# Compressed attention branch: three copies of the probabilities turned as one 128x128 piece, and one full-height product per query tile

## The chip, the cores and the metric

One NeuronCore of a Trainium2 chip runs the whole program. The metric is the device time of one execution in microseconds (us). Engines are named as the profile names them: PE (TensorE, matrix products and transposes; PEld is its weight load), DVE (VectorE), ACT (ScalarE), POOL (GpSimd), SP (SyncE, which issues most DMAs).

## The reference

Two layers over 256 tokens of width 2048: first an RWKV-7 mixer, then sparse attention with three branches (compressed, selected, window) over shared keys and values, each followed by an output product; a final norm ends it. The changed part is the compressed branch of the second layer: 16 heads in 4 groups, head width 128. Keys and values are compressed to 15 blocks, each query attends to the blocks that it can see, and the result is gated and added to the other branches:

```python
s = jnp.einsum('bgrqd,bgcd->bgrqc', qb, k_cmp).astype(jnp.float32) * scale      # c: 15 compressed blocks
vis = cmp_end[None, :] <= tq[:, None]
p_cmp = jax.nn.softmax(jnp.where(vis, s, NEG_INF), axis=-1) * jnp.any(vis, axis=-1)[:, None]
o_cmp = jnp.einsum('bgrqc,bgcd->bgrqd', p_cmp.astype(v_cmp.dtype), v_cmp)
...
o = gb[..., 0:1] * o_cmp + gb[..., 1:2] * o_sel + gb[..., 2:3] * o_win
```

With 256 tokens the selection takes all blocks, so the kernel computes the other two branches from the same causal scores with their own weights.

## The kernel before, in words

All products run in fp32r. An fp32 operand x is split into a high part (x rounded to fp32r by a copy on ACT) and a low part (x minus high, on DVE or POOL), and each product is the sum of three: high by high, high by low, low by high. Weights stream from DRAM through five raw buffers (line 176), are split on ACT (line 204) and on DVE or POOL (line 189), and are used by `rows_step` (lines 567 to 570; tokens stationary, up to 512 weight columns moving) and `cols_step` (lines 585 to 587; weights stationary, 256 tokens moving).

The stages in order: the RWKV layer; the shared keys and values (`phase_kv`, `compress`, buffers from the pool `kvp`); the attention stage, in which `phase_q` and `phase_z` stream the input weights while the attention of the heads runs beside them as a background generator; and the output product `phase_bo` with the final norm. When the attention stage opens, `kvp` is released and the pool `at` takes over its memory.

The order of instructions on each engine is not written by hand. The program is emitted in an order set by a small planner (`Sched`: each generator yields estimated costs in ns, and `sch.t` is the planned time), and the framework then orders each engine's queue by priority and by its own simulated time line. Calls through `Ranked` carry a priority offset; they all show as line 232 on PE, so their groups in the profile are told apart by tile names.

`compress(1, ...)` makes the compressed values: `vch` (high, ACT, line 1407) and `vcl` (low, DVE, line 1408), each 15 partitions by 4 groups by 128. `attend(p)` does one pair of heads, eight times, from pair 7 down to 0. For each head, `weigh` makes scores, exponentials (`P0`, `P1` for the causal scores, `Pc` for the compressed ones, two query tiles of 128 by 15) and scales them by gate and sum (lines 1527 to 1531). Then `turned` transposes four pieces into one PSUM bank and splits them into `Th` and `Tl` (512 columns: two heads by two query tiles by 128 queries), and `products` adds three products to the accumulator `o` (128 value rows by those 512 columns). T0, T1 and T2 serve the causal scores. T3 serves the compressed branch: four transposes of 128x15, `Th` and `Tl` of 15x512, and three products whose contraction has 15 rows:

```python
T3 = turned([Pc[:, t, 0:NCMP] for _, _, Pc in P for t in range(2)], NCMP)
...
products(o, (vch[:, g, :], vcl[:, g, :]), T3, stop=True)
```

Of the kernel before, what the change touches and what calls it, by code (L numbers as in the profile page):

```python
# [10 lines left out]
F32 = mybir.dt.float32  # L11
F32R = mybir.dt.float32r
AF = mybir.ActivationFunctionType
OP = mybir.AluOpType
# [9 lines left out]
NCMP = 15  # L24
GRP = 4
# [5 lines left out]
def _layout():  # L31
    p = np.arange(128)
    q = np.arange(64)
    f = {}
    f["ident"] = np.eye(128)
    f["bo"] = (p[:, None] // 64 == np.arange(2)[None])
    f["mi"] = (p % 64)[:, None] <= q[None]
    f["mst"] = (p % 64)[:, None] < q[None]
    f["rst"] = np.tile((np.arange(T) % CH != 0)[None], (128, 1))
    half_d = 16  # L40
    inv = (np.float32(500000.0) ** (-np.arange(half_d, dtype=np.float32) / np.float32(half_d))).astype(np.float32)
    pos = (np.arange(2)[None] * 128 + p[:, None]).astype(np.float32)
    ang = (pos[:, :, None] * inv[None, None]).astype(np.float32)
    f["cos"] = np.cos(ang.astype(np.float64)).reshape(128, 32)
    f["sin"] = np.sin(ang.astype(np.float64)).reshape(128, 32)
    angc = ((16.0 * (p % NCMP) + 31.0).astype(np.float32)[:, None] * inv[None]).astype(np.float32)
    f["ccos"] = np.cos(angc.astype(np.float64))
    f["csin"] = np.sin(angc.astype(np.float64))
    f["caus"] = np.where(p[None] <= p[:, None], 0.0, NEG)
    tt = np.arange(2)[None] * 128 + p[:, None]  # L50
    cend = 16 * np.arange(NCMP) + 31
    vis = cend[None, None] <= tt[:, :, None]
    f["vis"] = np.where(vis | ~vis.any(-1, keepdims=True), 0.0, NEG).reshape(128, 2 * NCMP)
    f["anyv"] = vis.any(-1)
    cols, parts, off = {}, [], 0
    for k, v in f.items():
        v = np.asarray(v, np.float32)
        cols[k] = (off, v.shape[1])
        parts.append(v)
        off += v.shape[1]  # L60
    return cols, np.ascontiguousarray(np.concatenate(parts, 1))
# [21 lines left out]
QTB, QB, PB, TB, OGB, RPB = 1, 8, 3, 3, 1, 1  # L83
# [132 lines left out]
def hybrid_kernel(ctx: ExitStack, tc: tile.TileContext, a: dict, out: bass.AP):  # L216
    nc = tc.nc
    V, S, G, PE = nc.vector, nc.scalar, nc.gpsimd, nc.tensor
    sch = Sched()
# [34 lines left out]
    def accp(name="acc"):  # L254
        n = turn.get(name, 0)
        turn[name] = n + 1
        b = role[name]
        return psum.tile([128, 512], F32, name=f"bank{b[n % len(b)]}", bufs=1)
# [104 lines left out]
    def C(name):  # L363
        o, n = COLS[name]
        return cst[:, o:o + n]
# [799 lines left out]
    for U in range(NU):  # L1165
        PBK[U] = pair_tile(U % 2)
        P = U - 1
# [54 lines left out]
    bp = kvp = xlp = None  # L1222
# [87 lines left out]
    KT = ktp.tile([128, GRP, 2, 272], F32, name="KT")  # L1310
    V.memset(KT[:, :, :, 256:], 0.0)
    Vt = [bp.tile([128, 2, GRP, 128], F32, name=f"Vt{i}") for i in range(2)]
    vcl = bp.tile([NCMP, GRP, 128], F32R, name="vcl")
    vch = bp.tile([NCMP, GRP, 128], F32R, name="vch")
    peT = bp.tile([128, 64], F32, name="peT")
    pt0 = accp("tp")
    PE.transpose(pt0[:, 0:64], perow, ident[:64, :64])
# [54 lines left out]
    def compress(j, o):  # L1372
        PE, V, S, G = Ranked(nc.tensor, "cpPE"), Ranked(nc.vector, "cpPE"), Ranked(nc.scalar, "cpPE"), Ranked(nc.gpsimd, "cpPE")
        t = kvp.tile([120, HID], F32, name="c1", bufs=1)
        S.activation(t, o, AF.Copy)
        pt = accp("tp")
        for m in range(2):
            PE.transpose(pt[:, m * 128:m * 128 + 120], t[:, m * 128:(m + 1) * 128], ident[:120, :120])
        yield 300.0
        p3 = pt[:, :256].rearrange("p (m c) -> p m c", m=2)  # L1380
        hs = kvp.tile([128, 2, 60], F32, name="c2", bufs=1)
        th = kvp.tile([128, 2, 60], F32, name="c3", bufs=1)
        S.activation(hs, p3[:, :, 60:120], AF.Copy)
        V.tensor_tensor(hs, p3[:, :, 0:60], hs, op=OP.add)
        S.activation(th, hs, AF.Tanh, scale=0.5)
        V.tensor_scalar(th, th, 0.5, 0.5, op0=OP.mult, op1=OP.add)
        V.tensor_tensor(hs, hs, th, op=OP.mult)
        yield 0.0
        o2 = accp("tp")
        if j == 0:  # L1390
            for m in range(2):
                PE.matmul(o2[:60, :128], hs[:, m, :], cw2[:, m, :], start=m == 0, stop=m == 1)
            kc = kvp.tile([128, 1, 1, 128], F32, name="kc", bufs=1)
            V.memset(kc, 0.0)
            S.activation(kc[:60, 0, 0, :], o2[:60, :128], AF.Copy)
            rope(kc, 1, C("ccos"), C("csin"), kvp, V)
            yield 0.0
            o3 = accp("tp")
            PE.transpose(o3[:, :60], kc[:60, 0, 0, :], ident[:60, :60])
            V.tensor_copy(KT[:, :, 0, 256:256 + NCMP], o3[:, :60].rearrange("p (g c) -> p g c", g=GRP))  # L1400
        else:
            for g in range(GRP):
                for m in range(2):
                    PE.matmul(o2[:NCMP, g * 128:(g + 1) * 128], hs[:, m, g * NCMP:(g + 1) * NCMP], cw2[:, 2 + m, :],
                              start=m == 0, stop=m == 1)
            vc = o2[:NCMP].rearrange("p (g d) -> p g d", g=GRP)
            S.activation(vch, vc, AF.Copy)
            V.tensor_tensor(vcl, vc, vch.bitcast(F32), op=OP.subtract)

    for ph in (phase_kv(0), phase_kv(2, 0), phase_kv(1), phase_kv(4, 1), phase_kv(3), phase_kv(5)):  # L1410
        sch.run(ph)
# [4 lines left out]
    at = tc.alloc_tile_pool(name="attn", bufs=1)  # L1416
# [5 lines left out]
    for tt in range(2):  # L1422
        rb = at.tile([128, 128], F32, name="rb", bufs=1)
        V.tensor_copy(rb, RS[tt].to_broadcast([128, 128]))
        PE.transpose(pr[:, tt * 128:(tt + 1) * 128], rb, ident)
    V.tensor_copy(RST, pr[:, :T])
    qd, zdone, kvd, used_q = {}, {}, {}, [0]

    def phase_q(n):
# [47 lines left out]
    def weigh(h):  # L1477
        PE, V, S, G = Ranked(nc.tensor, "atPE"), Ranked(nc.vector, "atE"), Ranked(nc.scalar, "atE"), Ranked(nc.gpsimd, "atE")
        g = h // GRP
# [28 lines left out]
        yield 500.0  # L1508
        P0 = at.tile([128, 2, 128], F32, name="P0", bufs=PB)
        P1 = at.tile([128, 2, 256], F32, name="P1", bufs=PB)  # L1510
        Pc = at.tile([128, 2, 16], F32, name="Pc", bufs=PB)
        for x in range(2):
            S.activation(P0[:, x], vA[:, x], AF.Exp, scale=SCALE, bias=mx[:, 0, x:x + 1], accum_out=sm[:, 0, x:x + 1])
        for t in range(2):
# [13 lines left out]
            V.tensor_scalar(P0[:, x], P0[:, x], rc[:, 0, x:x + 1], None, op0=OP.mult)  # L1528
            V.tensor_scalar(P1[:, x], P1[:, x], rc[:, 1, x:x + 1], None, op0=OP.mult)
        for t in range(2):  # L1530
            V.tensor_scalar(Pc[:, t, 0:NCMP], Pc[:, t, 0:NCMP], rc[:, t, 2:3], None, op0=OP.mult)
        yield 600.0
        return P0, P1, Pc

    def attend(p):
        PE, V, S, G = Ranked(nc.tensor, "atPE"), Ranked(nc.vector, "atE"), Ranked(nc.scalar, "atE"), Ranked(nc.gpsimd, "atE")
        g = p // 2
        if g not in kvd:
            split_kv(g)
        P = []  # L1540
        for h in (2 * p, 2 * p + 1):
            P.append((yield from weigh(h)))
        vh, vl = kvd[g][2:]

        def turned(pieces, n=128):
            pt = accp("PT")[:n]
            for i, piece in enumerate(pieces):
                PE.transpose(pt[:, i * 128:(i + 1) * 128], piece, ident)
            th = at.tile([128, 512], F32R, name="Th", bufs=TB)[:n]
            tl = at.tile([128, 512], F32R, name="Tl", bufs=TB)[:n]  # L1550
            S.activation(th, pt, AF.Copy)
            V.tensor_tensor(tl, pt, th.bitcast(F32), op=OP.subtract)
            sch.t += 430
            return th, tl

        def products(o, v, t, **kw):
            PE.matmul(o, v[0], t[0], start=kw.get("start", False), stop=False)
            PE.matmul(o, v[0], t[1], start=False, stop=False)
            PE.matmul(o, v[1], t[0], start=False, stop=kw.get("stop", False))

        T0 = turned([w for P0, P1, _ in P for w in (P0[:, 0], P1[:, 0, 0:128])])
        yield 500.0
        T1 = turned([w for P0, P1, _ in P for w in (P0[:, 1], P1[:, 1, 0:128])])
        yield 500.0
        if len(tails) >= OGB:
            yield lambda: ready(tails[0])
            yield from flush()
        o = accp("PV")
        os_ = o.rearrange("p (i s t) -> p i s t", i=2, s=2)[:, :, 1, :]
        products(o, (vh[:, 0, 0], vl[:, 0, 0]), T0, start=True)  # L1570
        T2 = turned([P1[:, x, 128:256] for x in range(2) for _, P1, _ in P])
        yield 500.0
        products(o, (vh[:, 1, 0], vl[:, 1, 0]), T1)
        T3 = turned([Pc[:, t, 0:NCMP] for _, _, Pc in P for t in range(2)], NCMP)
        yield 500.0
        for x in range(2):
            products(os_, (vh[:, x, 1], vl[:, x, 1]), [w[:, x * 256:(x + 1) * 256].rearrange("p (i t) -> p i t", i=2) for w in T2])
        products(o, (vch[:, g, :], vcl[:, g, :]), T3, stop=True)
        og = at.tile([128, 2, T], F32, name="og", bufs=OGB)
        S.activation(og, o.rearrange("p (i t) -> p i t", i=2), AF.Copy)  # L1580
        sch.t += 2600
        tails.append((p, og))
        yield 0.0
# [121 lines left out]
```

## Time and profile before

| | |
|---|---|
| runs before (us) | 1182.65, 1187.53, 1189.38; median 1187.53 |
| profiled execution: span from first to last instruction | 1181.0 us (the page gives no other time for it) |
| mean granted PE clock | 0.985 |
| PE busy | 1130.3 us (96%), 9416 instructions |
| DVE, ACT, POOL busy | 851.3 us (72%), 710.8 us (60%), 330.9 us (28%) |
| attention stage | from about 862 to 1085 us of the span |

How to read the profile's lines: a group shows line, engine, operation, output<-inputs by tile name, shape and count, then busy time and mean duration, and after the second bar the idle time of the engine just before, with what ended it. `bank` is any PSUM bank, `cst` the constants (the identity among them), `128*15` on a PE row the stationary operand's rows and columns and `128x512` the moving one's. In order of time a row begins with its start in the span and its length, in us. Matmuls overlap in these rows, since each is shown with its pipeline; how fast PE advances is read from start to start.

### The profile page before, as it was taken

The page shows a single profiled execution, that of the slowest core. Times are in us where ns is not written, and L with a number is a line of the kernel's source. Part 1 is how long each engine was busy: PE and PEld are TensorE (multiplying, and loading weights), DVE is VectorE, ACT ScalarE, POOL GpSimd, SP SyncE. Part 2 cuts the span into 40 slices and gives each one's busy share as a digit, 9 for nine tenths or more (in the row PEclk, how much of TensorE's full clock was granted, in tenths as well). Part 3 has the DMA queues.
Part 4 walks back from the last instruction along what each step waited for, and adds up shares of the span by engine and source line. Part 5 has one row for each costly group of instructions (what it writes and reads, how often), then busy time and mean ns, then how long its engine had stood idle before and what let it go on. Part 6 is the DMA issues. An engine that isn't in the chain of part 4 may idle for free.

```text
span 1181.0 us, 25607 instructions
## 1 busy us (share of the span) xinstructions
PE 1130.3 (96%) x9416; PEld 985.4 (83%) x9416; DVE 851.3 (72%) x1915; ACT 710.8 (60%) x1680; POOL 330.9 (28%) x413
## 2 busy tenths in 40 slices
PE   8999999999986999999989999999999999999997
PEld 7788899887965888888668888787989989989887
DVE  6999876589794876666655867674576888786564
ACT  5767777666762345565445867564656657665553
POOL 1300046234454255654000010100333233333011
PEclk8999999999997999999999999999999999999999
DMA  6558887786888669685355758585645353644752
GB/s 227 173 181 256 219 224 227 224 215 187 263 236 190 174 173 262 175 220 152 106 169 206 247 163 294 164 285 164 190 131 157 107 138 112 164 104 160 289 195 105
DMA packets 232765, 225.26 MB, mean 191 GB/s; under 512 B 51344, under 2 KB 180672, under 8 KB 232256
## 3 DMA queue, kind: packets, MB, share of 16 engines
q1 hardware_dynamic: 228000, 219.01, 61.8%
q0 software_dynamic: 4640, 4.62, 1.6%
q8 instruction: 74, 1.21, 0.4%
q14 instruction: 51, 0.42, 0.1%
HBM read 200.48 MB, written 23.10 MB: 189 GB/s over the span
## 4 chain that ended last, share of the span: by engine, by line
PE 76%; DVE 12%; DMA 4%; issue 4%; ACT 3%; POOL 2%; SPq 0%; ACTq 0%; POOLq 0%; DVEq 0%
PE bank L568 12%; PE bank L567 12%; PE bank L570 12%; PE bank L585 8%; PE bank L586 6%; PE bank L587 6%; PE bank L232 5%; DVE wlo L189 4%; PE pair L570 1%; PE pair L567 1%; PE pair L568 1%; DVE mtmp L424 1%; DVE ml L418 1%; PE pair L1046 1%; DVE invX L794 1%
## 5 line engine op out<-in xcount | busy, mean ns | idle before, releaser
L189 DVE TENSOR_TENSOR wlo<-wraw,whi 128x512 fp32r<-128x512 f32 (+2 forms) x616 | 441.9, 730 | 151.4 <-ACT whi L204 149.0
L204 ACT ACTIVATE whi<-wraw 128x512 fp32r<-128x512 f32 (+2 forms) x664 | 402.3, 619 | 199.3 <-PE bank L570 96.6
L585 PE MATMUL bank<-mh,whi 128*128 128x256 f32 (+1 forms) x800 | 239.7, 300 | 0.7 <-issue 0.7
L568 PE MATMUL bank<-wlo,mh 128*128 128x512 f32 (+3 forms) x608 | 230.2, 380 | 4.2 <-DVE wlo L189 4.2
L587 PE MATMUL bank<-mh,wlo 128*128 128x256 f32 (+1 forms) x800 | 228.6, 286 | 1.7 <-DVE wlo L189 1.7
L586 PE MATMUL bank<-ml,whi 128*128 128x256 f32 (+1 forms) x800 | 228.7, 286 | 0.0
L570 PE MATMUL bank<-whi,ml 128*128 128x512 f32 (+3 forms) x608 | 228.5, 378 | 0.0
L567 PE MATMUL bank<-whi,mh 128*128 128x512 f32 (+3 forms) x608 | 204.4, 381 | 0.9 <-ACT whi L204 0.9
L585 PEld LDWEIGHTS bank<-mh,whi 128*128 128x128 f32 (+1 forms) x800 | 152.3, 190 | 6.5 <-issue 0.9
L587 PEld LDWEIGHTS bank<-mh,wlo 128*128 128x128 f32 (+1 forms) x800 | 152.3, 191 | 3.2 <-DVE wlo L189 2.0
L586 PEld LDWEIGHTS bank<-ml,whi 128*128 128x128 f32 (+1 forms) x800 | 152.8, 191 | 2.2 <-issue 0.8
L568 PEld LDWEIGHTS bank<-wlo,mh 128*128 128x128 f32 x608 | 115.1, 189 | 22.5 <-DVE wlo L189 5.1
L567 PEld LDWEIGHTS bank<-whi,mh 128*128 128x128 f32 x608 | 114.6, 190 | 20.1 <-ACT whi L204 1.3
L570 PEld LDWEIGHTS bank<-whi,ml 128*128 128x128 f32 x608 | 114.8, 189 | 17.8 <-issue 0.4
L189 POOL TENSOR_TENSOR wlo<-wraw,whi 128x512 fp32r<-128x512 f32 (+2 forms) x48 | 62.6, 1305 | 190.1 <-ACT whi L204 158.3
L568 PE MATMUL bank<-wlo,kvh 128*128 128x512 f32 x192 | 77.0, 401 | 0.0
L570 PE MATMUL bank<-whi,kvl 128*128 128x512 f32 x192 | 76.1, 396 | 0.0
L567 PE MATMUL bank<-whi,kvh 128*128 128x512 f32 x192 | 67.4, 396 | 0.0
L417 ACT ACTIVATE mh<-mtmp 128x256 fp32r<-128x256 f32 x96 | 38.9, 413 | 27.2 <-DVE mtmp L424 25.6
L424 DVE SCALAR_TENSOR_TENSOR mtmp<-xx,prm,xn 128x256 f32<-128x256 f32 x96 | 47.8, 510 | 1.2 <-POOL xx L456 1.0
L715 POOL TENSOR_TENSOR sp<-an,pinv 64x256 f32<-64x256 f32 x32 | 36.3, 1133 | 34.1 <-DVE an L710 32.6
L1035 ACT ACTIVATE X<-pair 128x128 f32<-128x128 f32 x32 | 8.9, 279 | 58.5 <-PE pair L1033 35.9
(325 smaller groups left out, 1909.3 us busy)
## 6 DMA issues: line engine op xcount, KB each, us to landing
wraw<-in_a_w_rkvz_dram SPq DMA_DIRECT2D x128, 512.0 KB, 4.9
wraw<-in_kv_w_dram SPq DMA_DIRECT2D x48, 512.0 KB, 4.5
wraw<-in_b_w_in_dram SPq DMA_DIRECT2D x40, 512.0 KB, 4.0
wraw<-in_a_w_o_dram SPq DMA_DIRECT2D x32, 512.0 KB, 4.1
wraw<-in_b_w_o_dram SPq DMA_DIRECT2D x32, 512.0 KB, 3.7
spd<-sp SPq DMA_DIRECT2D x16, 642.0 KB, 4.7
spl<-spd SPq DMA_DIRECT2D x16, 642.0 KB, 5.6
wraw<-in_b_w_in_dram SPq DMA_DIRECT2D x24, 384.0 KB, 3.2
```

The costliest lines, as they stand in the source:

```text
L189: eng.tensor_tensor(lv, src, hv.bitcast(F32), op=OP.subtract)
L204: self.nc.scalar.activation(hv, src, AF.Copy)
L232: return fn(*args, **kw)
L417: S.activation(h, src, AF.Copy)
L424: V.scalar_tensor_tensor(m, xx[:, k, :], mu[:, k:k + 1], xn[:, k, 1:], op0=OP.mult, op1=OP.add)
L567: PE.matmul(o, mh[:, ts], wh[:, 0, :], start=k == ends[0], stop=False)
L568: PE.matmul(o, mh[:, ts], wl[:, 0, :], start=False, stop=False)
L570: PE.matmul(o, ml[:, ts], wh[:, 0, :], start=False, stop=k == ends[1])
L585: PE.matmul(o, wh[:, s, :], mh, start=k == 0 and first, stop=False, **kw)
L586: PE.matmul(o, wh[:, s, :], ml, start=False, stop=False, **kw)
L587: PE.matmul(o, wl[:, s, :], mh, start=False, stop=k == NK - 1, **kw)
L715: G.tensor_tensor(BK[r, :, h, :], c3(an)[r], c3(pinv)[r], op=OP.mult)
```

## The change

- The probabilities of a head go into a tile of 128 columns: two query tiles by four slots of 16. The scaling on DVE writes the same 15 values into three of the slots (slot four and the sixteenth column stay zero; two such tiles per head of a pair, zeroed once, alternate). `Pc` itself now has two buffers.
- One 128x128 transpose per head replaces two of 128x15. On the turned rows, ACT makes a rounded copy and DVE one scalar_tensor_tensor with a constant column `lom` (-1 on the second slot's rows, else 0): the first and third slot hold the rounded probabilities, the second the low part.
- The values stand once in a tile `vst` of 128 rows: rows of query tile t hold high, high, low, and the rest is zero. It is zeroed by POOL, its first slot is written by ACT, and five DMAs on POOL's queue copy the other slots from `vch` and from `vcl`, which now lies in `kvp`.
- One product of 128 rows and 256 columns (both heads) per query tile replaces the three of 15 rows and 512 columns: two per pair instead of three.
- The planner's clock advances in `turned` by 215 for T3 instead of 430.

```diff
+    f["lom"] = -1.0 * (p % 64 // 16 == 1)[:, None]
...
-    vcl = bp.tile([NCMP, GRP, 128], F32R, name="vcl")
-    vch = bp.tile([NCMP, GRP, 128], F32R, name="vch")
+    vst = bp.tile([128, 2, GRP, 128], F32R, name="vst")
+    G.memset(vst.bitcast(F32), 0.0)
...
+            vch = vst[0:NCMP, 0]
+            vcl = kvp.tile([NCMP, GRP, 128], F32R, name="vcl")
             S.activation(vch, vc, AF.Copy)
             V.tensor_tensor(vcl, vc, vch.bitcast(F32), op=OP.subtract)
+            for t in range(2):
+                for c, src in enumerate((vch, vch, vcl)):
+                    if t or c:
+                        o = 64 * t + 16 * c
+                        G.dma_start(vst[o:o + NCMP, t], src)
...
+    PCC = [at.tile([128, 2, 2, 4, 16], F32, name=f"pcc{i}") for i in range(2)]
+    for t in PCC:
+        G.memset(t, 0.0)
...
-        Pc = at.tile([128, 2, 16], F32, name="Pc", bufs=PB)
+        Pc = at.tile([128, 2, 16], F32, name="Pc", bufs=2)
+        Pcc = PCC[h // 2 % 2][:, h % 2]
...
-            V.tensor_scalar(Pc[:, t, 0:NCMP], Pc[:, t, 0:NCMP], rc[:, t, 2:3], None, op0=OP.mult)
+            V.tensor_scalar(Pcc[:, t, 0:3, 0:NCMP], Pc[:, t, None, 0:NCMP].to_broadcast([128, 3, NCMP]),
+                            rc[:, t, 2:3], None, op0=OP.mult)
         yield 600.0
-        return P0, P1, Pc
+        return P0, P1, Pcc.rearrange("p t c n -> p (t c n)")
...
-        def turned(pieces, n=128):
-            pt = accp("PT")[:n]
+        def turned(pieces, cmp=False):
+            n = 128 * len(pieces)
+            pt = accp("PT")[:, :n]
             for i, piece in enumerate(pieces):
                 PE.transpose(pt[:, i * 128:(i + 1) * 128], piece, ident)
-            th = at.tile([128, 512], F32R, name="Th", bufs=TB)[:n]
-            tl = at.tile([128, 512], F32R, name="Tl", bufs=TB)[:n]
+            th = at.tile([128, 512], F32R, name="Th", bufs=TB)[:, :n]
+            tl = at.tile([128, 512], F32R, name="Tl", bufs=TB)[:, :n]
             S.activation(th, pt, AF.Copy)
-            V.tensor_tensor(tl, pt, th.bitcast(F32), op=OP.subtract)
-            sch.t += 430
+            if cmp:
+                V.scalar_tensor_tensor(tl, th.bitcast(F32), C("lom"), pt, op0=OP.mult, op1=OP.add)
+            else:
+                V.tensor_tensor(tl, pt, th.bitcast(F32), op=OP.subtract)
+            sch.t += n * 0.84
...
-        T3 = turned([Pc[:, t, 0:NCMP] for _, _, Pc in P for t in range(2)], NCMP)
+        T3 = turned([Pcc for _, _, Pcc in P], True)[1].rearrange("p (i t) -> p i t", i=2)
...
-        products(o, (vch[:, g, :], vcl[:, g, :]), T3, stop=True)
+        for t in range(2):
+            PE.matmul(o.rearrange("p (i s t) -> p s i t", i=2, s=2)[:, t], vst[:, t, g, :], T3, start=False, stop=t == 1)
```

## The prediction

> **What bounds the kernel now.** I read the page first (busy time of each engine, the chain that ended last), then busy time by stage, then the order of time on TensorE in the attention stage.
>
> ```profile
> span 1181.0 us, 25607 instructions
> PE 76%; DVE 12%; DMA 4%; issue 4%; ACT 3%; POOL 2%; SPq 0%; ACTq 0%; POOLq 0%; DVEq 0%
> ```
>
> TensorE (PE) carries the chain, and no other engine more than 12%. A busy PE is a share over stages, and its ends are modelled, so the next table is by stage; its columns are stretch, length, busy time (instructions) of PE, weight load, DVE, ACT and POOL, granted clock, DMA share, GB/s.
>
> ```profile
> 862.00:1085.00 223.00, 222.09 (x1501) 204.59 (x1500) 170.83 (x476) 142.85 (x412) 76.50 (x69) 1.00 0.47 130
> 1085.00:1181.00 96.00, 88.02 (x480) 76.62 (x478) 53.04 (x82) 45.84 (x86) 13.33 (x12) 0.97 0.55 198
> ```
>
> The attention stage, where the edited lines run eight times (once for each pair of heads), is 862 to 1085. PE is busy for 222.09 of 223.00 us, at full clock (1.00). What PE waited for there, in all (us, times, longest):
>
> ```profile
> PE bank L1449 <- DVE qt L1308: 0.9, 1, 0.9
> ```
>
> So in this stage the time is the sum of what each PE instruction holds the array, and a microsecond saved on PE moves the end by a microsecond unless another engine becomes late. What an instruction holds is not its duration (they overlap) but the distance from its start to the next start.
>
> **The change, part by part.** First the three 15-row products of each of the eight pairs, which become two products of 128 rows and 256 columns. PE in order of time (start us, duration), at the first pair and at the last, where other work stands between them:
>
> ```profile
> 894.52 0.28 PE L232 MATMUL bank<-Tl,vh 128*128 128x256 f32 x1
> 894.64 0.28 PE L232 MATMUL bank<-Th,vl 128*128 128x256 f32 x1
> 894.84 0.50 PE L232 MATMUL bank<-Th,vch 15*128 15x512 f32 x1
> 895.18 0.39 PE L232 MATMUL bank<-Tl,vch 15*128 15x512 f32 x1
> 895.42 0.39 PE L232 MATMUL bank<-Th,vcl 15*128 15x512 f32 x1
> 895.74 0.44 PE L567 MATMUL bank<-whi,mh 128*128 128x384 f32 x1
> 896.02 0.34 PE L568 MATMUL bank<-wlo,mh 128*128 128x384 f32 x1
> 896.19 0.34 PE L567 MATMUL bank<-whi,mh 128*128 128x384 f32 x1
> ...
> 1076.31 0.28 PE L587 MATMUL bank<-mh,wlo 128*128 128x256 f32 x1
> 1076.52 0.50 PE L232 MATMUL bank<-Th,vch 15*128 15x512 f32 x1
> 1076.94 0.39 PE L585 MATMUL bank<-mh,whi 128*128 128x256 f32 x1
> 1077.17 0.28 PE L586 MATMUL bank<-ml,whi 128*128 128x256 f32 x1
> ...
> 1077.64 0.28 PE L587 MATMUL bank<-mh,wlo 128*128 128x256 f32 x1
> 1077.85 0.49 PE L232 MATMUL bank<-Tl,vch 15*128 15x512 f32 x1
> 1078.18 0.39 PE L232 MATMUL bank<-Th,vcl 15*128 15x512 f32 x1
> 1078.51 0.39 PE L585 MATMUL bank<-mh,whi 128*128 128x256 f32 x1
> 1078.73 0.28 PE L586 MATMUL bank<-ml,whi 128*128 128x256 f32 x1
> ```
>
> A 256-column product holds the array 0.12 us (894.52 to 894.64); a 384-column one 0.17 (896.02 to 896.19). Standing together, the three cost 896.02 - 894.64 = 1.38 less the neighbours' 0.12 and 0.17: 1.09 us. Standing apart they cost (1077.17 - 1076.31 = 0.86, less two neighbours, 0.62) and (1078.73 - 1077.64 = 1.09, less two, 0.85): 1.47 us. Each place where the number of rows changes takes about 0.1 us on both sides (0.21 instead of 0.12 ahead of Th,vch; the next start after a lone Th,vch comes at 0.42). Worked out in this way at all eight pairs: 1.09 and 1.10 where they stand together, 1.30 to 1.49 at the six where other instructions come between; 10.5 us in all. Bounds: eight of the first kind 8.7, eight of the last 11.8.
>
> What replaces them has 128 rows like its neighbours, so I take the 128-row price of 0.12: 16 x 0.12 = 1.9 us. Their output has the same strides as the products just ahead of them (256 of 512 columns, every second block). The lower end is that; the upper end, if both sides of each group paid a change as now, 8 x 0.2 more, 3.5 us. I take 1.9, since nothing changes its number of rows. Gain on this part 8.6 us (between 5.2 and 9.9).
>
> Next the turning: four transposes of 15 columns become two of 128 columns. PE at the last pair:
>
> ```profile
> 1072.44 0.39 PE L232 MATMUL bank<-Tl,vh 128*128 128x512 f32 x1
> 1072.67 0.27 PE L232 MATMUL bank<-cst,Pc 128*15 128x128 f32 x1
> 1072.69 0.48 PE L232 MATMUL bank<-Th,vl 128*128 128x512 f32 x1
> 1073.01 0.49 PE L232 MATMUL bank<-cst,Pc 128*15 128x128 f32 x3
> 1073.26 0.37 PE L586 MATMUL bank<-ml,whi 128*128 128x256 f32 x1
> 1073.46 0.28 PE L587 MATMUL bank<-mh,wlo 128*128 128x256 f32 x1
> ```
>
> 1073.46 - 1072.44 = 1.02, less two 512-column products of 0.23 (1072.44 to 1072.67) and one of 0.12, leaves 0.44 for four: 0.11 each, scattered or not. The wider transposes stream the same 128 columns of the identity, and I price them the same: 8 x 2 x 0.11 = 1.8 us gained (bounds 0, if a wide one took twice as long, and 1.8).
>
> A rule against the first part's price is in the Trainium skill. "TensorE: Matmul & The Clock Gate", section "Why this matters for your kernels", says that a single product with 32 rows takes the same time as one with 128 rows. By it the three small products would be worth three 512-column ones, and the sum below would halve; the rows speak against it, since a lone one holds the array 0.42 where it would be the 0.23 of a 512-column product.
>
> Now the other engines. VectorE: the low half on 15x512 becomes one scalar_tensor_tensor on 128x256 from PSUM, and the scaling writes 45 elements instead of 15. ScalarE: the high copy goes from 512 columns to 256. Busy us and mean ns, or durations min/median/max in ns:
>
> ```profile
> L1552 DVE TENSOR_TENSOR Tl<-bank,Th 15x512 fp32r<-15x512 f32 x8 | 5.4, 673 | 1.6 <-ACT Th L1551 1.6
> L1272 DVE SCALAR_TENSOR_TENSOR kvl<-bank,prm,kvh x16: 473/479/485, 652.1 to 688.8; 128x256 fp32r<-128x256 f32 x16
> L1531 DVE TENSOR_SCALAR Pc<-Pc,rc x32: 215/224/1277, 871.7 to 1065.5; 128x15 f32<-128x15 f32 x32
> L1441 DVE SCALAR_TENSOR_TENSOR gl<-bank,rsh,gbias x2: 267/268/270, 852.9 to 853.3; 128x48 f32<-128x48 f32 x2
> ```
>
> VectorE: 8 x (0.48 - 0.67) = -1.5 us and 32 x (0.27 - 0.22) = +1.6, about nothing; ScalarE gets eight shorter copies. Both lie beside PE (170.83 and 142.85 of 223.00), so they count zero; bounds: nothing to a gain of 1 us where VectorE is late now (its 0.9 above). The added wait: the first of the new products needs the low half, where the first old one needed only the high half. Behind it on PE stands everything else; whether it comes late is the second rival.
>
> Once only, outside the loop: two kinds of fills on GpSimd (one of 128x1024, two of 128x256), five copies on its DMA queue after the compressed values are ready, one more constant column in a load that is made anyway.
>
> ```profile
> L755 POOL MEMSET invT<- 128x1024 f32 x1 | 1.0, 955 | 2.9 <-DMA tnd<-invT 2.9
> 704.62 2.67 POOL L1347 TENSOR_TENSOR cx<-cxt,cx 128x480 fp32r<-128x480 f32 x2 [25.17 <-ACT cx L1346]
> L1408 DVE TENSOR_TENSOR vcl<-bank,vch x1: 679/679/679, 806.2 to 806.2; 15x512 fp32r<-15x512 f32 x1
> gbias<-in_b_gate_b_dram POOLq DMA_DIRECT2D x1, 24.0 KB, 3.9
> 827.92 1.12 POOL L189 TENSOR_TENSOR wlo<-wraw,whi 128x432 fp32r<-128x432 f32 x1 [61.04 <-ACT whi L204]
> 832.95 0.35 DVE L1424 COPY rb<-rsh 128x128 f32<-128x128 f32 x1 [1.67 <-PE bank L570]
> ```
>
> The large fill takes about 1 us and falls in the 25 us in which GpSimd has nothing ahead of 704.62; the small ones, a quarter of that each by size, come among its weight halves near 833 (an idle stretch of a few us stands between those). The copies start at 806.2 + 0.7 = 806.9, in the 61 us in which GpSimd has nothing ahead of 827.92, so nothing queues behind them; if each took a whole 3.9 us after the one before, they would be down at 826.4, before the attention's buffers open (832.95) and long before the first reader (894.84). All of it counts zero, between 0 and 1 us of loss.
>
> Sum: 8.6 + 1.8 = 10.4 us less, between 4 (5.2 + 0 - 1) and 13 (9.9 + 1.8 + 1). Against the profiled execution: 1181.0 - 10.4 = 1170.6 us of span. The page gives no other time for this execution; its span is 6.5 us below the median of the three runs (1187.53), and I carry this distance: 1187.5 - 10.4 = 1177.1 us. After the attention stage nothing gives it back: between 1085 and 1170 PE goes on being busy (88.02 of 96.00, the rest is the closing tail), so the end moves as a block.
>
> **The rivals.**
>
> *PE pays by columns alone* (the page's rule above). The 15-row products would be worth 3 x 0.23 a pair, 5.5 us in all, and the gain 5.5 - 1.9 + 1.8 = 5.4: 1182.1 us. Speaking against it: the 0.34 and 0.42 to the next start in the quoted rows. Chance 0.04.
>
> *VectorE becomes late and takes part of it back.* In one pair the low half is ready close before its product, in order of time on VectorE and then on PE:
>
> ```profile
> 959.95 0.67 DVE L1552 TENSOR_TENSOR Tl<-bank,Th 15x512 fp32r<-15x512 f32 x1
> 961.09 0.50 PE L232 MATMUL bank<-Th,vch 15*128 15x512 f32 x1
> ```
>
> 0.47 us lie between 960.62 and 961.09, and no pair is closer than that. PE would go through the stage 10 us sooner with the same VectorE work: 171 of 213 us, 80% instead of 77. That still leaves room on average, so I give it the loss of half the gain, some 5 us, by waits at the pairs that lie so close, and the order of instructions, laid out anew, could do as much: 1182 us. It decides if PE's waits in the stage grow from 0.9 to over 5. Chance 0.17.
>
> *Slower: the copies hold the attention's buffers back.* The low part of the compressed values now lies in a buffer of the stage before, whose memory the attention stage takes over at 832.95. PE would stand until the last copy has read it. It costs more than the gain if the copies end over 10.4 us late, at 843.4, and shows as slower by 0.5% at 849.3. From 806.9 that is 42 us for five copies of 30 KB, where one of 24 KB took 3.9; I price it at twice 10.4 lost: 1198 us. Chance 0.06.
>
> **How the numbers follow.** Half a percent, about what a measurement of this kernel can tell from no change, is 5.9 us. The forecast holds 0.73 (by itself 1172 to 1181), nearly all of it faster by over 0.5%; the column rule 0.04 and the late VectorE 0.17 end within 0.5%, though the latter at times just outside on the fast side; the copies 0.06 slower. Faster 0.74, same 0.20, slower 0.06. The three runs before lie 6.7 us apart (1182.65 to 1189.38), so the range takes the sum's upper bound of 13 with some of that below, 1169, and reaches over the second rival above, 1186.
>
> **What would show it.** Right: no 15-row product; 16 products of 128x256 on the new tile, starting 0.12 us before their successor; 16 transposes at 0.11; PE's count down by 24; the last PE instruction of the attention stage about 10 us earlier; PE's waits there about 1 us as before. Wrong: a PE wait for the low half or a weight half in the stage, a start distance of 0.2 or more at the new products, or a gap on PE near 833 that ends with a DMA.

## The result, and the profile after

| | before | after |
|---|---|---|
| median of 20 runs (us) | 1187.15 (1182.65 to 1192.01) | 1181.86 (1176.76 to 1185.09) |
| ratio | 1 | 0.9949 (95%: 0.9936 to 0.9962) |
| span of the profiled execution (us) | 1181.0 | 1181.7 |

The kernel became faster by 0.5%, by the ratio 6.1 us at 1187.15 (the two medians alone lie 5.3 apart), where 10.4 was forecast. The two spans alone would show nothing, for the profile of before was one of the quickest executions. The attention's buffers open (the transposes of line 1425 before, 1433 after) at 833.36 us before and at 840.12 after, though up to there the programs differ by one fill, five copies and a constant; in the nine kernels profiled for this text the same point lies between 832.8 and 840.1. So I count from that point to the last instruction: 347.6 us before, 341.5 after, 6.1 less, which is what the twenty runs say.

The page after, the counterparts of the lines of before:

```profile
span 1181.7 us, 25564 instructions
PE 72%; DVE 13%; DMA 5%; issue 4%; ACT 3%; POOL 2%; SPq 1%; ACTq 0%; POOLq 0%; DVEq 0%
```

By stage, before and then after: from the opening to the last `og`, and on to the last PE instruction (columns as in the prediction):

```profile
833.36:1078.70 245.34, 244.43 (x1624) 226.13 (x1625) 184.25 (x506) 156.63 (x441) 83.62 (x74) 1.00 0.50 138
1078.70:1172.70 94.00, 94.00 (x530) 82.77 (x530) 55.06 (x82) 47.79 (x89) 14.51 (x13) 1.00 0.55 196
```

```profile
840.12:1081.40 241.28, 237.21 (x1618) 225.79 (x1619) 191.41 (x510) 156.09 (x444) 83.56 (x76) 1.00 0.53 141
1081.40:1173.40 92.00, 92.00 (x513) 80.72 (x513) 52.66 (x79) 46.26 (x86) 14.17 (x13) 1.00 0.57 196
```

PE's busy time in the stage fell by 7.2 us and the stage by only 4.1: PE now stands still for 4.1 us of it, where it stood 0.9 before. VectorE's busy time rose by 7.2 us for four instructions more. What PE waited for in the stage after (the last column is the longest wait):

```profile
PE bank L569 <- DVE wlo L190: 2.0, 2, 1.3
PE bank L233 <- DVE ql L1464: 1.2, 1, 1.2
PE bank L588 <- DVE wlo L190: 0.9, 1, 0.9
```

The new products and transposes at the last pair, in order of time:

```profile
1076.73 0.39 PE L233 MATMUL bank<-Tl,vh 128*128 128x512 f32 x1
1076.96 0.27 PE L233 MATMUL bank<-cst,pcc 128*128 128x128 f32 x1
1076.98 0.48 PE L233 MATMUL bank<-Th,vl 128*128 128x512 f32 x1
1077.30 0.27 PE L233 MATMUL bank<-cst,pcc 128*128 128x128 f32 x1
1077.33 0.36 PE L588 MATMUL bank<-mh,wlo 128*128 128x256 f32 x1
1077.53 0.28 PE L586 MATMUL bank<-mh,whi 128*128 128x256 f32 x1
...
1080.75 0.28 PE L586 MATMUL bank<-mh,whi 128*128 128x256 f32 x1
1080.87 0.40 PE L233 MATMUL bank<-Tl,vst 128*128 128x256 f32 x2
1081.11 0.28 PE L587 MATMUL bank<-ml,whi 128*128 128x256 f32 x1
```

The two products hold the array 0.24 us between two neighbours, with nothing lost on either side; the transposes take 1077.53 - 1076.73 = 0.80 less 0.23, 0.23 and 0.12, so 0.11 each. Both as priced.

One of the places where PE stands, on PE, VectorE and GpSimd:

```profile
952.10 0.51 PE L568 MATMUL bank<-whi,mh 128*128 128x384 f32 x2
953.87 0.44 PE L569 MATMUL bank<-wlo,mh 128*128 128x384 f32 x1 [1.26 <-DVE wlo L190]
...
949.15 1.08 DVE L1540 TENSOR_SCALAR P<-P,rc 128x128 f32<-128x128 f32 x1
950.16 0.84 DVE L1541 TENSOR_SCALAR P<-P,rc 128x256 f32<-128x256 f32 x1
950.92 0.75 DVE L1540 TENSOR_SCALAR P<-P,rc 128x128 f32<-128x128 f32 x1
951.60 1.11 DVE L1541 TENSOR_SCALAR P<-P,rc 128x256 f32<-128x256 f32 x1
952.63 0.39 DVE L1543 TENSOR_SCALAR pcc<-Pc,rc 128x45 f32<-128x45 f32 x2
952.95 0.40 DVE L1475 SCALAR_TENSOR_TENSOR zT<-zth,zT 128x256 f32<-128x256 f32 x1
953.27 1.01 DVE L190 TENSOR_TENSOR wlo<-wraw,whi 128x384 fp32r<-128x384 f32 x2
...
949.14 1.01 POOL L190 TENSOR_TENSOR wlo<-wraw,whi 128x384 fp32r<-128x384 f32 x1 [3.11 <-ACT whi L205]
950.11 1.48 POOL L1615 TENSOR_TENSOR ml<-og,mh 128x256 fp32r<-128x256 f32 x2
951.55 1.01 POOL L190 TENSOR_TENSOR wlo<-wraw,whi 128x384 fp32r<-128x384 f32 x1
```

Each of the four scalings of P starts just after an instruction of GpSimd has begun and ends just after it (949.14 + 1.01 = 950.15, the scaling 950.23; 951.55 + 1.01 = 952.56, the scaling 952.71). Elsewhere in this trace the same instructions take 0.28 and 0.34 us:

```profile
1017.89 0.28 DVE L1540 TENSOR_SCALAR P<-P,rc 128x128 f32<-128x128 f32 x1
1018.09 0.34 DVE L1541 TENSOR_SCALAR P<-P,rc 128x256 f32<-128x256 f32 x1
```

So VectorE comes 2.5 us late (3.78 us for four that need 1.24) to the weight half for which PE stands from 952.6. The other three places (977, 989 and 1019 us) have held-up instructions of VectorE ahead of them in the same way. The two groups of scalings over the attention stage, before and after:

```profile
L1528 DVE TENSOR_SCALAR P<-P,rc 128x128 f32<-128x128 f32 x32 | 10.9, 341 | 0.0
L1529 DVE TENSOR_SCALAR P<-P,rc 128x256 f32<-128x256 f32 x32 | 17.5, 547 | 0.0
```

```profile
L1540 DVE TENSOR_SCALAR P<-P,rc 128x128 f32<-128x128 f32 x32 | 15.5, 486 | 0.0
L1541 DVE TENSOR_SCALAR P<-P,rc 128x256 f32<-128x256 f32 x32 | 18.5, 579 | 0.0
```

So 5.6 of the 7.2 us more on VectorE lie in these 64 instructions. Taken one by one, each of them lasts either 0.27 to 0.35 us or over 0.7, and every one of the second kind overlaps an instruction of GpSimd. Before, 11 of the 64 are held up, after, 19.

VectorE was thus held up in the kernel before as well. The one wait of PE that the prediction shows there (0.9 us for `qt`) comes about in this way, behind a low half of a weight that takes 1.73 us, where one of the same size takes 0.68 at 968.42:

```profile
970.67 1.73 DVE L189 TENSOR_TENSOR wlo<-wraw,whi 128x512 fp32r<-128x512 f32 x1
972.49 0.25 DVE L1308 TENSOR_TENSOR qt<-rp,rp 128x96 f32<-128x96 f32 x1
...
970.56 1.29 POOL L189 TENSOR_TENSOR wlo<-wraw,whi 128x512 fp32r<-128x512 f32 x1 [0.86 <-ACT whi L204]
```

To say where the time went I compare each distance from one PE start to the next, from the opening to the last PE instruction, with the undisturbed price of its columns (0.229 us for 512, 0.174 for 384, 0.119 for 256, 0.108 for a transpose and so on). What exceeds the price by over 0.2 us is a stall; the rest is small losses, the changes of rows above all. In us:

| kernel | total | priced work | small losses | stalls |
|---|---|---|---|---|
| before | 339.4 | 332.4 | 5.9 | 1.1 |
| after | 333.3 | 327.1 | 1.5 | 4.7 |
| padded rows (experiment 1) | 338.0 | 332.4 | 1.4 | 4.3 |
| padded rows, scaling on ScalarE (2) | 333.3 | 332.4 | 0.9 | 0 |
| after, scaling on ScalarE (3) | 327.8 | 327.1 | 0.8 | 0 |
| before, scaling on ScalarE (4) | 339.3 | 332.4 | 6.4 | 0.5 |
| after, without GpSimd's low halves (5) | 328.0 | 327.1 | 0.9 | 0 |
| before, without GpSimd's low halves (6) | 338.2 | 332.4 | 5.8 | 0 |
| after, with 80 more transposes (7) | 342.0 | 335.7 | 1.9 | 4.4 |

The change took 5.3 us of work and 4.4 of small losses from PE, 9.7 in all, and 3.6 us of stalls came back. Of the four kernels in which VectorE does the scalings beside all of GpSimd's work, the one with 11 held-up scalings stalls for 1.1 us, and those with 17 to 19 (experiment 1: 17, experiment 7: 18, after: 19) for 4.3 to 4.7.

### The profile page after: what moved, and what is told of

The parts are those of the page before. It is cut to its first block, busy times and chain, and to the rows that moved or that the text cites. A ratio compares the mean times of both kernels' runs of the same rounds, so it can differ in the third digit from the quotient of the medians.

```text
span 1181.7 us, 25564 instructions
## 1 busy us (share of the span) xinstructions
PE 1126.2 (95%) x9392; PEld 987.1 (84%) x9392; DVE 856.0 (72%) x1915; ACT 709.7 (60%) x1680; POOL 332.9 (28%) x421
## 4 chain that ended last, share of the span: by engine, by line
PE 72%; DVE 13%; DMA 5%; issue 4%; ACT 3%; POOL 2%; SPq 1%; ACTq 0%; POOLq 0%; DVEq 0%
PE bank L569 12%; PE bank L571 12%; PE bank L568 12%; PE bank L586 7%; PE bank L588 6%; PE bank L587 6%; DVE wlo L190 4%; PE bank L233 4%; PE pair L571 1%; PE pair L568 1%; PE pair L569 1%; DVE mtmp L425 1%; DMA abd<-abs 1%; DVE invX L795 1%; PE pair L1047 1%
```

## The experiments

The theory: PE's saving is as forecast, and GpSimd's instructions hold up VectorE just ahead of operands that PE needs. The rivals: the rows cost nothing and the saving was never there; VectorE simply has too much to do beside a faster PE; the microseconds went elsewhere.

**1. Rows alone.** The kernel before, padded with zeros to 128 rows: `Pcc` has 128 columns, zero but for 15, and `vcl` and `vch` have 128 rows, zeroed once, of which 15 are written. The transposes take 128 columns with it, and `Pc` has two buffers as in the changed kernel.

```diff
-        T3 = turned([Pc[:, t, 0:NCMP] for _, _, Pc in P for t in range(2)], NCMP)
+        T3 = turned([Pcc[:, t] for _, _, Pcc in P for t in range(2)])
...
-    vcl = bp.tile([NCMP, GRP, 128], F32R, name="vcl")
+    vcl = bp.tile([128, GRP, 128], F32R, name="vcl")
...
```

> The kernel before, with the compressed branch padded by zeros to 128 rows: still four transposes (now 128 columns wide) and three products of 512 columns a pair. Only the number of rows changes. Theory (a change of rows costs TensorE about 0.1 us on each side): 24 products at 0.23 us, 5.5 us in all in place of 10.5, so the cost of the branch's products falls by 5.0 us, about 1182 us against 1187. Rival (TensorE pays by columns alone): the products cost the same 5.5 us as the rival says they did before, no difference in time, 1187 us.

Measured: ratio 0.9977 (0.9957 to 0.9996), 1184.8 us. PE at the last pair, where the same products stand apart:

```profile
1075.65 0.28 PE L587 MATMUL bank<-mh,wlo 128*128 128x256 f32 x1
1075.77 0.40 PE L232 MATMUL bank<-Th,vch 128*128 128x512 f32 x1
1076.00 0.28 PE L585 MATMUL bank<-mh,whi 128*128 128x256 f32 x1
...
1076.59 0.28 PE L587 MATMUL bank<-mh,wlo 128*128 128x256 f32 x1
1076.71 0.39 PE L232 MATMUL bank<-Tl,vch 128*128 128x512 f32 x1
1076.94 0.40 PE L232 MATMUL bank<-Th,vcl 128*128 128x512 f32 x1
1077.17 0.28 PE L585 MATMUL bank<-mh,whi 128*128 128x256 f32 x1
```

0.23 each, 0.12 ahead of them, some 5.5 us at the eight pairs in place of 10.5: the price of the rows is shown, and the rule that columns alone count does not hold here. The time fell by only 2.7 us, because stalls rose from 1.1 to 4.3; the longest are three waits for VectorE of 0.7 to 1.1 us, one of them again behind a scaling held up to 1.05 us by an instruction of GpSimd.

**2. The same with the scaling of P0 and P1 on ScalarE.** The edit of experiment 3 on the kernel of experiment 1.

> The kernel before with the compressed branch padded to 128 rows (three products of 512 columns, four transposes), and the scaling of P0 and P1 on ScalarE. Theory (a change of rows costs what the rows of the trace show, and only waits for VectorE hid it when the padding was tried alone): no stalls, 5.0 us for the rows and 1 us for the old wait, 1181 us; products at 5.4 us in the trace. Rival (the padding is worth only the 2.7 us that it showed alone): 1184 us.

Measured: ratio 0.9950 (0.9929 to 0.9971), 1181.4 us, no stall, some 5.5 us for the products. Against the kernel before that is 5.9 us, of which the old stall is 1.1. Against experiment 4, which has the scaling on ScalarE and 15 rows, it is 0.9950 / 0.9974 = 0.9976, 2.9 us by the ratios (4.2 by the medians), and 6.0 in the table. The times alone don't settle whether the rows are worth 3 us or 6, and the intervals of experiments 1 and 2 just overlap; the trace carries the point.

**3. After, with the scaling on ScalarE.**

```diff
-            V.tensor_scalar(P0[:, x], P0[:, x], rc[:, 0, x:x + 1], None, op0=OP.mult)
-            V.tensor_scalar(P1[:, x], P1[:, x], rc[:, 1, x:x + 1], None, op0=OP.mult)
+            S.activation(P0[:, x], P0[:, x], AF.Copy, scale=rc[:, 0, x:x + 1])
+            S.activation(P1[:, x], P1[:, x], AF.Copy, scale=rc[:, 1, x:x + 1])
```

> The changed kernel, with the scaling of P0 and P1 moved from VectorE to ScalarE (64 instructions, some 34 us less on VectorE, some 25 us more on ScalarE). Theory (GpSimd's instructions hold up VectorE's scalings just ahead of weight halves that TensorE needs): the scalings can no longer be held up, TensorE's waits for VectorE in the attention stage fall from 4.1 us to under 1, and the time falls by some 4 us, to about 1178. Rival (the missing 4 us went elsewhere, for instance into the order of TensorE's instructions): the waits may go, but the time stays at 1182. Second rival (ScalarE then comes late): waits for ScalarE in place of those for VectorE, 1182 or more.

Measured: ratio 0.9884 (0.9858 to 0.9909), 1175.4 us, the best kernel of this study, below before and after, and 5.5 us below after in the table. All that PE waited for from the opening on, and the stage by engines:

```profile
PE bank L1433 <- DVE rb L1432: 0.5, 1, 0.5
...
832.80:1067.40 234.60, 234.60 (x1607) 224.34 (x1608) 167.87 (x444) 176.40 (x507) 81.39 (x76) 1.00 0.53 144
```

PE is busy for the whole stage; the one wait is at its opening. ScalarE's 20 us more stay beside PE. VectorE also has less to do here, so this experiment alone can't tell the hold-ups from too much work; experiments 5 and 6 can.

**4. Before, with the scaling on ScalarE.** The same edit.

> The kernel before, with the scaling of P0 and P1 on ScalarE, as was done to the changed kernel. Theory (the change saves about 10 us of TensorE's work, and VectorE's lateness takes some 4 back): this kernel loses its 1 us of waits and no more, about 1186 us, and the changed kernel with the same move (1175.4 us) lies the full 10 us below it. Rival (the move itself is worth those microseconds in either kernel): it gains 6 us here too, 1181 us, and the distance stays at 6.

Measured: ratio 0.9974 (0.9955 to 0.9993), 1185.6 us. The move is worth little by itself (3.1 us by the ratio, with an interval of 0.8 to 5.3, and 0.1 in the table); between experiments 4 and 3 lie 0.9884 / 0.9974 = 0.9910, some 10.7 us by the ratios, and 11.5 in the table of totals. With VectorE out of the way the change gives what was forecast. The two were not timed side by side but on two chips, each against the kernel before, so this quotient has no interval of its own; their two intervals together allow an estimated 4 us either way.

**5 and 6. Without GpSimd's low halves of weights.** VectorE keeps its scalings. The products take the high half in place of the low halves that GpSimd made, so these two kernels leave out a part of the result.

```diff
-            self.due.append((lv, src, hv, eng))
+            if self.split in self.on_pool:
+                lv = hv
+            else:
+                self.due.append((lv, src, hv, eng))
```

> The changed kernel without the 48 low halves of weights that GpSimd computes: the products take the high half twice in their place, so TensorE, VectorE and ScalarE do the same work, and GpSimd some 60 us less. Theory (GpSimd holds up VectorE): VectorE's stretched instructions shrink, by some 20 us of busy time in the attention stage, TensorE's waits there fall under 1.5 us, time about 1178. Rival (VectorE has too much work beside a faster TensorE, whatever GpSimd does): waits and time as in the changed kernel, 1182.

> The same omission in the kernel before (GpSimd's 48 low halves of weights replaced by the high half). Theory: TensorE waited only 1 us in its attention stage, so at most 1 us is gained, 1186 us, and the distance to the changed kernel with the same omission is the full 10 us of the prediction. Rival: the distance stays at 6 us.

Measured: after 0.9890 (0.9865 to 0.9914), 1175.5 us; before 0.9980 (0.9962 to 0.9998), 1185.7 us. The scalings of the changed kernel in this experiment, and the stage:

```profile
L1544 DVE TENSOR_SCALAR P<-P,rc 128x128 f32<-128x128 f32 x32 | 9.5, 296 | 0.0
...
835.94:1072.40 236.46, 236.46 (x1621) 226.28 (x1622) 169.90 (x510) 157.30 (x444) 22.14 (x29) 1.00 0.53 145
```

VectorE does the same instructions (510 in the stage, as after) in 169.9 us instead of 191.4, and PE no longer stands. The rival of too much work for VectorE falls: the work is the same, and GpSimd's falls from 83.6 us to 22.1. The distance between the two kernels is 10.2 us in the table, and 0.9890 / 0.9980 = 0.9910 by the ratios, where it is 6 us with GpSimd's halves. The intervals allow some 4 us either way here too; the stalls in the table, none in either kernel, carry the point.

**7. After, with a slower PE.**

```diff
-            for i, piece in enumerate(pieces):
+            for i, piece in list(enumerate(pieces)) * (6 if cmp else 1):
```

> The changed kernel with the two transposes of the compressed probabilities done six times over into the same place: 80 more transposes of 0.11 us, 8.7 us of TensorE's work, nothing else. Theory A (VectorE's lateness shows because TensorE comes sooner): with TensorE as slow as before the stalls of 4.7 us shrink to 1 or 2, and the time rises by only 5 to 6 us, to about 1187.5. Theory B (the stalls come from how the order of instructions fell out, whatever TensorE's speed): the stalls stay at 4 to 5 us and the time rises by the full 8.7, to about 1190.5.

Measured: ratio 1.0015 (0.9993 to 1.0037), 1190.8 us; 8.6 us more priced work, stalls 4.4, some for ScalarE as well. In the stage:

```profile
PE bank L588 <- DVE wlo L190: 1.4, 1, 1.4
PE bank L569 <- DVE wlo L190: 1.2, 2, 0.7
```

This speaks for theory B: in this kernel a PE as slow as before does not hide VectorE's lateness. (The added work let the framework lay out the order anew, as in every kernel here, so PE's speed was not changed alone.)

What stays open is why the new order meets GpSimd more often (19 scalings instead of 11). All of the framework's order after the first edited line is laid out anew, and the experiments do not tell which edit moves the scalings against GpSimd's instructions. The planner's 215 instead of 430 is not it: with that edit undone, each engine's list of instructions is the same.

## Why the prediction was right or wrong

The time lies in the stated range (1169 to 1186), which reaches over the second rival, and just outside the 1172 to 1181 that the forecast had by itself: of its 10.4 us 6.1 came. PE's side of the sum was right, and VectorE's side was wrong. One of the signs that the prediction gave for being wrong, a wait of PE for a weight half in the stage, is in the trace after (2.0 and 0.9 us for `wlo`).

- *The products* (8.6 us): right. 10.5 before, 1.9 after (eight pairs at 0.24), 8.6 gained.
- *The transposes* (1.8 us): right, 0.11 each, wide or narrow; 16 fewer.
- *The column rule* (rival, 0.04): refuted by experiment 1.
- *The copies and fills* (zero; the slow rival): right. The copies were issued from 813.3 to 815.9 and landed within 4.2 us each; PE's wait at the opening is 0.5 us for `rb`, as in the kernel before.
- *VectorE counts zero, at best a gain of 1 us*: this is the step that failed. The prices were right (0.47 us for the new low half, as the row of line 1272 said), but the term had no bound on the side of a loss, and PE's stalls rose by 3.6 us. The cover was read from a share (171 of 223 us busy), while the row of line 1531 stood in the prediction's own fence with 215, 224 and a largest of 1277 ns: an instruction that at times takes five times its length, for no wait of its own. Durations on VectorE were taken as fixed; those of the scalings and of the weights' low halves hang on what GpSimd does at that moment. The 0.9 us that PE waited before was already such a case, and the prediction did not ask what had made `qt` late.
- *The second rival* (VectorE takes back half, 0.17) is what happened, at nearly its price (5 us forecast, 3.6 found), but not by its main reason. It blamed the faster PE and the low half of T3; experiment 7 speaks against PE's speed, and no wait for `Tl` stands in the trace after. It also named the order laid out anew, with no price or mechanism of its own, and that is the part that the runs leave standing. Its own sign, waits of over 5 us, was not reached (4.1). That the time came out at 1181.9, next to its 1182, is in part luck.
- *The distance of 6.5 us* between the span and the median was carried as if it belonged to the kernel. Some 1.9 us of it stand between time and span in the profiled execution after as well (1183.56 against 1181.7). The rest belongs to the execution: the profile of before was near the quick end of runs that spread over 9.4 us. The gain forecast does not depend on it.

## What to carry to other kernels

A product of 15 rows among 128-row ones cost more here than its columns: read the distance from start to start on both sides of it, and pad or stack to full height where the engine is the bound. Where a saving on one engine rests on another that is "busy for 77%", look at the largest durations of that engine's instructions and not only at their sum: a maximum of five times the median says that something holds it up, and whether that comes just ahead of a needed operand changes with each new order. Before judging a change of half a percent by two profiles, find a point that both programs reach with the same work, and count from there.

## What the runs showed of the hardware

- A scaling on VectorE that reads and writes SBUF in fp32 is held up while GpSimd works: 1.08 instead of 0.28 us, and it ends 0.1 us after GpSimd's instruction. A low half of a weight, with two inputs in SBUF, is held up as well: 1.73 instead of 0.68 us. In the kernel after, PE's stalls were 3.6 us longer than before through such hold-ups, though neither engine was the bound. In the Trainium skill, "SBUF — State Buffer", section "SBUF: two separate sides", says that VectorE and GpSimd share a pair of ports under an exclusive lock, and that the later of the two waits for the other's whole instruction, where VectorE's runs in a two-port mode or has two inputs in SBUF. The trace agrees on the waiting: in the rows quoted, VectorE's instruction begins 0.01 to 0.11 us after GpSimd's and ends after it. No row here shows in which mode a scaling runs.
- TensorE lost about 0.1 us at each change between 128 and 15 rows, and nothing of the kind between products of 128 rows. In the trace before, the weight load of the lone 15-row product and the next 128-row one begin only with their own products (1076.52 and 1076.94); between products of 128 rows the load begins 0.12 us ahead of its product (1077.05 and 1077.17).
